# A one-layer hybrid decoder step: Pool's weight subtraction in halves, more store buffers, other pacer costs, ordering edges, and another scheduling simulation

## The chip, the cores and the metric

The kernel runs on one core of a Trainium2 chip. The metric is device microseconds of the whole program from launch to end. TensorE (PE) does the matrix products; VectorE (DVE), ScalarE (ACT) and GpSimd (POOL) do elementwise work; the DMAs that matter here are issued one after another by SyncE (SP). Each engine works through its own list of instructions in order and waits on semaphores for the others.

## The reference

One layer of a decoder for 2048 prompt tokens and 8 sequences of 8 new tokens, all in float32, model width 1024:

```python
h = rmsnorm(x, norm_attn)
p = h @ w_in                                   # 1024 -> q, k, v, 14 RWKV slices, 2048 gates
o_attn = attention(q, k, v)                    # sliding window of 128, with sinks
o_rwkv = rwkv7_mixer(p[..., e3:e4], ...)       # a linear recurrence over time, state 64 x 64 a head
merged = g1 * (o_attn @ w_branch_attn) + g2 * (o_rwkv @ w_branch_rwkv)
x = x + merged @ w_out
u = rmsnorm(x, norm_ffn) @ w_ffn_in            # 1024 -> 2 * 2816
f = (gelu(causal_conv3(gate)) * value) @ w_ffn_out
y = rmsnorm(x + f, norm_final)
```

The outputs are y for both sets of tokens and the new caches: window keys and values, the last RWKV row, the RWKV state and the last convolution rows.

## The kernel before, in words

**Tiling.** The 2112 tokens are three blocks of 704, each worked on in two halves of 384 and 320 columns (`HALF`). Activations lie with the channel on the 128 partitions. A float32 product is made from three products in a reduced float32 format: weights and activations are split in a high and a low part, and `mm3` (line 321) does high x high, low x high, high x low for each 128 rows of the contraction. One weight unit is 128 x 1024; `unit` (line 301) loads it into `wr` (two buffers), ACT copies it to the high part (L310), and for two units in three POOL, for the third DVE, subtracts to get the low part (L313) in `wp` (two buffers). A unit feeds 48 matmuls: three times eight, for each half.

**Stages.** `run` goes through: `inputs(0)` (the projections of block 0), `inputs(1)`, the merge of block 0 (`merge`: branch products, `w_out`, second norm), its feed-forward part (`ffn`), `inputs(2)`, merge and `ffn` of block 1, merge and `ffn` of block 2. These dense products are the foreground. Each half's product ends in a PSUM bank of the pool `psd` (three banks) that DVE or ACT empties: L767 and L772 in the projections, L1277 and L1303 in the merge, L1337 and L1344 (`up`, `gb`) and L1373 in `ffn`.

**The background.** Everything of a block that isn't a dense product is a Python generator, pushed onto a named stream. `prep` (stream r) forms the operands of the recurrence and ends in six PSUM evacuations (two of ACT into `kt`, then four of DVE into `m`), whose tiles share one tag with two buffers and are each stored by a DMA (L914 to L939). `rest(b)` (stream c) runs `inverse` twice (a triangular inverse: 31 pairs of DVE instructions L1016 and L1018, then five DVE transposes L1022 and L1027, then small matmuls), beside it the attention of the block, then the recurrence `chain` in 11 chunks and its group norm. `rest(0)` runs under `inputs(1)`, `rest(1)` and `rest(2)` under the two first `ffn` stages. `drain` forces out what is left of a stream where a stage needs its result.

**What sets the order.** Before each 128-row step of a dense product `mm3` calls `tick` (line 262), which offers every stream one step of its generator. The pacer decides by clocks of its own: `cost` (line 213) gives each traced instruction a price, `account` (line 236) adds it up for each engine, and `step` (line 268) goes on only if no engine's clock is more than `ROOM` ahead of PE's and if the stream's due time is past. A generator's `yield 0.2` sets the due time 0.2 us behind the modelled end of its step. So the pacer's prices set after which dense matmul each background instruction is traced. The library then puts each engine's instructions in order with a simulation of its own, by priority (the order of tracing) and readiness; an instruction that is ready earlier in the simulation may come ahead of one traced before it.

Of the kernel before, what the change touches and what calls it, by code (L numbers as in the profile page):

```python
# [17 lines left out]
P = 128  # L18
# [9 lines left out]

ROOM = {"DVE": 2.0, "Activation": 2.5, "Pool": 4.0}
LAG = tuple((j, h) for j in range(6) for h in range(2)) + ((6, 0), (7, 0), (6, 1), (7, 1))  # L30
# [72 lines left out]
class Kernel:  # L103
    def __init__(self, tc, i, o, es):
# [13 lines left out]
        self.clock = dict.fromkeys(("PE", "DVE", "Activation", "Pool"), 0.0)  # L118
        self.seen, self.chained = 0, 0.0

# [5 lines left out]

    def bank(self, k="r"):
        return self.pb[k].tile([P, 512], F32, tag="ps" + k, name="ps" + k)

# [82 lines left out]
    @staticmethod  # L212
    def cost(ins, engine):
        n = 1
        for _, k in ins.outs[0].ap[1:]:
            n *= k
        if engine == "PE":
            if ins.ins[0].dtype == F32R:
                return 0.013 + 0.00042 * n
            if ins.is_transpose or n <= 2:  # L220
                return 0.11
            return 0.01 + 0.00168 * n / (1 if min(ins.tile_size) == P else 2)
        kind = type(ins).__name__
        if engine == "Activation":
            return 0.19 + 0.00084 * n
        two = kind == "InstTensorTensor"
        if engine == "Pool":
            return 0.1 + (0.0024 if two else 0.0009) * n
        if kind == "InstStreamTranspose":
            return 0.06 + 0.002 * n  # L230
        full = [a for a in ins.ins if hasattr(a, "ap") and math.prod(k for _, k in a.ap[1:]) > 1]
        if len(full) > 1 and not any(a.bass_ap.tensor.name.startswith("ps") for a in full):
            return 0.1 + 0.0014 * n
        return 0.1 + (0.00105 if len(full) > 1 else 0.0009) * n

    def account(self):
# [4 lines left out]
        for k in range(self.seen, m):  # L241
            ins = new[k]
            engine = str(ins.engine).split(".")[-1]
            if engine not in t or not type(ins).__name__.startswith("Inst") or isinstance(ins, mybir.InstDMACopy):
                continue
            c = self.cost(ins, engine)
            if engine == "PE":
                t["PE"] += c
                self.chained = max(self.chained, t["PE"] + 0.1)
            else:  # L250
                t[engine] = max(t[engine], t["PE"]) + c
                self.chained = max(self.chained + c + 0.06, t[engine])
        self.seen = m
        return self.chained

    def push(self, stream, *gens):
        self.streams.setdefault(stream, deque()).extend([g, 0.0, 0.0] for g in gens)

    def tick(self):

        self.account()
        for q in self.streams.values():
            self.step(q)

    def step(self, q):
        t = self.clock
        if not q or q[0][1] > t["PE"] or any(t[e] - t["PE"] > r for e, r in ROOM.items()):
            return
        self.account()
        entry = q[0]  # L270
        self.chained = max(entry[2], t["PE"])
        try:
# [3 lines left out]
            w = None  # L276
        end = self.account()
        if isinstance(w, tuple):
            entry[1], entry[2] = w[0], 0.0
        else:  # L280
            entry[1], entry[2] = (0.0, end) if w is None else (end + w, 0.0)

    def together(self, *queues):

        qs = [deque([g, 0.0, 0.0] for g in q) for q in queues]
        while any(qs):
# [4 lines left out]
    def drain(self, *names):  # L291

        while any(self.streams.get(n) for n in names):
            self.account()
            for n in names:
                q = self.streams.get(n)
                if q:
                    self.clock["PE"] = max(self.clock["PE"], q[0][1], *(self.clock[e] - r for e, r in ROOM.items()))
                    self.step(q)
# [3 lines left out]
    def unit(self, src, w=None):  # L303
# [8 lines left out]
        self.nw += 1  # L312
        eng.tensor_tensor(w[:, 1], raw, w[:, 0].bitcast(F32), op=ALU.subtract)  # L313
        return w
# [504 lines left out]
    def prep(self, b, p, hf, xk, xv, xr, pp, st):  # L819
# [90 lines left out]
        for u in range(0, nch, 4):  # L910
# [3 lines left out]
            for c in range(k):  # L914
                nc.tensor.transpose(ps[:, c * 128:(c + 1) * 128], kb[:, u + c], self.cst("ident"))
            kt = pp.tile([P, 4, 128], F32, tag="m", name="kt", bufs=2)
            nc.scalar.copy(kt[:, :k].rearrange("p c j -> p (c j)"), ps[:, :k * 128])
            nc.sync.dma_start(self.kbd[b][hf][u:u + k, :, p].rearrange("c q j -> q c j"), kt[:, :k])

        for u in range(0, nch, 4):  # L920
# [8 lines left out]
            for r_ in range(2):  # L929
                ps = pss[r_]  # L930
                m = pp.tile([P, 4, 128], F32, tag="m", name="m", bufs=2)
                kpr = k
# [3 lines left out]
                if kpr:  # L936
                    nc.vector.tensor_tensor(m[:, :kpr], ps[:, :kpr * 128].rearrange("p (c j) -> p c j", j=128),  # L937
                                            self.cst("maskp").unsqueeze(1).to_broadcast([P, kpr, 128]), op=ALU.mult)
                nc.sync.dma_start(self.md[b][hf][u:u + k, :, p, r_].rearrange("c q j -> q c j"), m[:, :k])  # L939

    def headsum(self, sq, sel, least, eps, k):
# [42 lines left out]
    def inverse(self, b, hf, ip):  # L984
# [38 lines left out]
        for r in range(2):  # L1023
            o = 64 - r * 64
            for u in range(2):
                rows = slice(o + 32 * u, o + 32 * u + 32)
                nc.vector.transpose(q[rows, :, 32 * u:32 * u + 32].rearrange("p b t -> p t b"), qb[rows])  # L1027
            nc.gpsimd.memset(q[o + 32:o + 64, :, 0:32], 0.0)
# [488 lines left out]
    def rest(self, b):  # L1517

        with self.pool("att", side="right") as ap:
            att = [self.attn_prompt(b, ap)]  # L1520
            if b == NB - 1:
                att.append(self.attn_sample(ap))
            yield from self.together([self.inverse(b, hf, ap) for hf in range(2)], att)
        with self.pool("chain", 2, side="right") as kp:
# [162 lines left out]
```

## Time and profile before

| what | us |
|---|---|
| median of three runs | 3515.13 (3509.72 to 3517.71) |
| the profiled execution | 3505.69 |
| its span, first to last instruction | 3503.6 |
| PE busy | 3309.8 (94%) |
| DVE busy | 2061.3 (59%) |
| ACT busy | 1232.9 (35%) |
| POOL busy | 928.1 (26%) |

Idle time of PE is the span less its busy time. A group of instructions is given by its line, engine, operation, and written tile `<-` read tiles; `psd` is a foreground PSUM bank, `psr` and `psc` are background banks. A wait reads "engine tile line <- engine tile line": the instruction that stood still and the one that let it go. PEclk is the share of the full TensorE clock that was granted.

### The profile page before, as it was taken

What the parts mean: (1) busy time and instruction counts of PE and PEld (TensorE: products, weight loads), DVE (VectorE), ACT (ScalarE), POOL (GpSimd) and SP (SyncE); (2) the same over time, 40 slices, a digit from 0 to 9 for tenths busy, and PEclk for the clock granted to TensorE, in tenths of its full rate; (3) what the DMA queues carried; (4) which work ended last, traced back from release to release, by engine and by line L of the source; (5) the groups of instructions that cost most, each with busy time, mean ns of one, the idle gap of its engine ahead of it and who ended that gap; (6) DMA issues with size and microseconds to landing.
All of it is one profiled execution on the core that took longest, in us unless ns stands there. A gap on an engine that the chain in (4) does not pass through costs nothing.

```text
span 3503.6 us, 60421 instructions
## 1 busy us (share of the span) xinstructions
PE 3309.8 (94%) x24072; PEld 3163.1 (90%) x24072; DVE 2061.3 (59%) x4088; ACT 1232.9 (35%) x2276; POOL 928.1 (26%) x632
## 2 busy tenths in 40 slices
PE   8999899998989899999999998989999999999998
PEld 8889888887989889999899998988899999999997
DVE  6566777533567755575665256775455565555555
ACT  4233344522233462332333323355222323222223
POOL 3233232211332121122333243221212243122123
PEclk9999999998999999999999999999999999999999
DMA  4455354465432226432644642322632272222222
GB/s 129 129 164 152 112 136 141 116 203 181 140 90 79 72 82 182 142 106 67 199 128 137 192 143 75 84 76 82 183 113 95 81 239 89 67 67 68 72 67 72
DMA packets 341834, 416.02 MB, mean 119 GB/s; under 512 B 110896, under 2 KB 269488, under 8 KB 341296
## 3 DMA queue, kind: packets, MB, share of 16 engines
q1 hardware_dynamic: 337392, 406.39, 38.2%
q10 hardware_dynamic: 4160, 5.77, 0.5%
q8 instruction: 189, 3.10, 0.4%
q14 instruction: 93, 0.76, 0.1%
HBM read 314.63 MB, written 98.41 MB: 118 GB/s over the span
## 4 chain that ended last, share of the span: by engine, by line
PE 59%; DVE 11%; DMA 4%; issue 4%; ACT 2%; POOL 2%; SPq 1%; DVEq 0%; POOLq 0%; ACTq 0%
PE psd L326 51%; DVE qt L1016 2%; DVE cc L1347 2%; DVE qb L1018 1%; DVE qinv L1027 1%; POOL wp L313 1%; ACT wp L310 1%; DMA kbd<-kt 1%; DVE ff L318 1%; PE psr L678 1%; PE psr L630 1%; PE psc L1090 1%; DVE wp L313 1%; PE psc L1123 0%; PE psc L1120 0%
## 5 line engine op out<-in xcount | busy, mean ns | idle before, releaser
L326 PE MATMUL psd<-o,wp 128*128 128x320 f32 (+1 forms) x7488 | 1280.2, 329 | 61.8 <-DVE gb L1344 18.4
L326 PEld LDWEIGHTS psd<-o,wp 128*128 128x128 f32 x7488 | 1223.2, 191 | 85.2 <-issue 29.2
L326 PE MATMUL psd<-h,wp 128*128 128x384 f32 (+1 forms) x6336 | 1126.5, 332 | 34.5 <-ACT wp L310 13.9
L326 PEld LDWEIGHTS psd<-h,wp 128*128 128x128 f32 x6336 | 1037.3, 192 | 57.3 <-ACT wp L310 14.9
L313 POOL TENSOR_TENSOR wp<-wr,wp 128x1024 fp32r<-128x1024 f32 x236 | 572.0, 2424 | 1754.2 <-ACT wp L310 1587.0
L310 ACT CAST wp<-wr 128x1024 fp32r<-128x1024 f32 x354 | 371.4, 1049 | 578.3 <-PE psd L326 525.3
L326 PE MATMUL psd<-ff,wp 128*128 128x384 f32 (+1 forms) x3168 | 536.5, 326 | 4.6 <-DVE ff L318 2.7
L326 PEld LDWEIGHTS psd<-ff,wp 128*128 128x128 f32 x3168 | 511.5, 188 | 13.7 <-issue 5.8
L1373 DVE TENSOR_TENSOR x<-x,psd 128x320 f32<-128x320 f32 (+1 forms) x288 | 148.7, 519 | 227.1 <-PE psd L326 226.2
L1347 DVE SCALAR_TENSOR_TENSOR cc<-gb,pt,cc 128x704 f32<-128x704 f32 (+1 forms) x132 | 190.0, 1439 | 34.2 <-ACT cc L1345 32.9
L313 DVE TENSOR_TENSOR wp<-wr,wp 128x1024 fp32r<-128x1024 f32 x118 | 145.5, 1233 | 63.7 <-ACT wp L310 62.6
L1345 ACT ACTIVATE cc<-gb,pt 128x64 f32<-128x64 f32 (+2 forms) x154 | 96.2, 638 | 243.2 <-DVE gb L1344 233.4
L1344 DVE TENSOR_TENSOR gb<-psd,rb 128x64 f32<-128x64 f32 (+2 forms) x154 | 70.2, 469 | 169.7 <-PE psd L326 169.4
L318 DVE TENSOR_TENSOR ff<-cc,ff 128x384 fp32r<-128x384 f32 (+1 forms) x132 | 115.2, 875 | 43.2 <-ACT ff L317 43.1
L1356 ACT ACTIVATE cc<-cc 128x704 f32<-128x704 f32 x66 | 52.4, 794 | 177.7 <-DVE cc L1347 102.2
L367 POOL TENSOR_TENSOR acc<-acc,sq 128x320 f32<-128x320 f32 (+1 forms) x81 | 82.6, 1021 | 86.1 <-ACT sq L366 83.5
L317 ACT CAST ff<-cc 128x384 fp32r<-128x384 f32 (+1 forms) x132 | 63.9, 488 | 99.0 <-DVE cc L1359 97.9
L1337 DVE TENSOR_TENSOR up<-psd,rb 128x384 f32<-128x384 f32 (+1 forms) x132 | 68.5, 519 | 50.1 <-PE psd L326 50.1
L1283 DVE SCALAR_TENSOR_TENSOR h<-m,h 128x384 fp32r<-128x384 f32 (+1 forms) x48 | 51.9, 1081 | 66.3 <-ACT h L1282 66.3
L937 DVE TENSOR_TENSOR m<-psr,ct 128x512 f32<-128x512 f32 (+2 forms) x88 | 45.7, 539 | 76.0 <-DMA kbd<-kt 57.5
L1016 DVE TENSOR_TENSOR qt<-nb,qb 128x31 f32<-128x31 f32 (+15 forms) x186 | 85.7, 461 | 4.5
L1280 POOL TENSOR_TENSOR m<-m 128x384 f32<-128x384 f32 (+1 forms) x48 | 48.2, 1004 | 149.9 <-DVE m L1277 103.9
(256 smaller groups left out, 3274.1 us busy)
## 6 DMA issues: line engine op xcount, KB each, us to landing
wr<-in_w_fi SPq DMA_DIRECT2D x132, 512.0 KB, 3.5
wr<-in_w_in SPq DMA_DIRECT2D x108, 512.0 KB, 3.8
wr<-in_w_fo SPq DMA_DIRECT2D x66, 512.0 KB, 3.5
cm<-md SPq DMA_DIRECT2D x33, 512.0 KB, 4.7
gt<-gd SPq DMA_DIRECT2D x48, 352.0 KB, 3.5
md<-m SPq DMA_DIRECT2D x48, 256.0 KB, 2.8
wr<-in_w_br SPq DMA_DIRECT2D x24, 512.0 KB, 3.9
wr<-in_w_out SPq DMA_DIRECT2D x24, 512.0 KB, 3.5
```

The source lines that it names most:

```text
L310: nc.scalar.copy(w[:, 0], raw)
L313: eng.tensor_tensor(w[:, 1], raw, w[:, 0].bitcast(F32), op=ALU.subtract)
L317: self.nc.scalar.copy(hi, src)
L318: (eng or self.nc.vector).tensor_tensor(lo, src, hi.bitcast(F32), op=ALU.subtract)
L326: nc.tensor.matmul(ps[:, :n], w[:, a, wk * 128:(wk + 1) * 128], act[:, k0 + k, b, c0:c0 + n], start=(start and k == 0 and j == 0), stop=(s ...
L367: eng.tensor_tensor(acc, acc, sq[:, :n], op=ALU.add)
L1016: nc.vector.tensor_tensor(tv, nb[:, s + 1:, s:s + 1].to_broadcast([P, k, s + 1]), qb[:, s:s + 1, :s + 1].to_broadcast([P, k, s + 1]), op=A ...
L1337: nc.vector.tensor_tensor(up[:, c0:c0 + n], ps[:, :n], rb[:, c0:c0 + n], op=ALU.mult)
L1344: nc.vector.tensor_tensor(dst, view(ps, 0), view(rb, c0), op=ALU.mult)
L1345: nc.scalar.activation(view(c, c0), dst, ACT.Identity, bias=self.par("cb", f), scale=cw[2])
L1347: nc.vector.scalar_tensor_tensor(c[:, :npr], gb[:, u:u + npr], cw[u], c[:, :npr], op0=ALU.mult, op1=ALU.add)
L1373: nc.vector.tensor_tensor(xv, xv, ps[:, :n], op=ALU.add)
```

## The change

It has six parts.

1. POOL's subtraction of a weight unit is done in two instructions of 512 columns; DVE's stays one of 1024.
2. `kt` and `m` have four buffers for blocks 0 and 2; for block 1 the first pair of `m` keeps two, and `kt` and the second pair of `m` borrow the two tiles of the tag `xv`.
3. The pacer's prices change: ACT's fixed part falls from 0.19 to 0.12; DVE instructions with two full inputs cost 0.0012 a column wherever these lie; small matmuls cost in proportion to the used part of the array; matmuls of one or two columns cost 0.223. A DVE instruction that reads no PSUM and would begin during a POOL two-input instruction is priced to begin near that one's end. ACT's `ROOM` falls from 2.5 to 2.0.
4. The pacer waits for more: a step needs the second of the last three modelled ends of `psr` use to be past, each named wait is 0.3 longer, a stream can have a least distance between steps (1.4 for `inverse`), and the four transposes of L1027 each get a step of their own.
5. Every background instruction on DVE and ACT is ordered behind the last foreground instruction on its engine that reads `psd` and was traced before it. It is an order in the engine's list and no semaphore.
6. The library's ordering pass runs on its timeline simulation (`schedule_with_timeline_sim=True`) instead of its default one.

```diff
@@
-ROOM = {"DVE": 2.0, "Activation": 2.5, "Pool": 4.0}
+ROOM = {"DVE": 2.0, "Activation": 2.0, "Pool": 4.0}
...
+        self.anchor, self.inside = {}, False
+        self.seen, self.chained, self.free = 0, 0.0, deque([0.0] * 3, 3)
+        self.taken, self.locked = 0, (0.0, 0.0)
...
     def bank(self, k="r"):
+        self.taken += k == "r"
...
             if ins.ins[0].dtype == F32R:
-                return 0.013 + 0.00042 * n
-            if ins.is_transpose or n <= 2:
-                return 0.11
-            return 0.01 + 0.00168 * n / (1 if min(ins.tile_size) == P else 2)
+                return 0.0135 + 0.000417 * n
+            if ins.is_transpose:
+                return 0.11 * n / 128
+            if n <= 2:
+                return 0.223
+            return max(0.03, 0.01 + 0.00168 * n * math.prod(ins.tile_size) / (P * P))
...
-            return 0.19 + 0.00084 * n
+            return 0.12 + 0.00084 * n
...
-            return 0.06 + 0.002 * n
+            return 0.06 + 0.0019 * n
...
-        if len(full) > 1 and not any(a.bass_ap.tensor.name.startswith("ps") for a in full):
-            return 0.1 + 0.0014 * n
-        return 0.1 + (0.00105 if len(full) > 1 else 0.0009) * n
+        return 0.1 + (0.0012 if len(full) > 1 else 0.0009) * n
...
+            if engine in ("DVE", "Activation"):
+                if self.inside:
+                    if engine in self.anchor:
+                        self.tc.add_manual_dep(ins, self.anchor[engine], mybir.DependencyInfo(
+                            mybir.DependencyClass.NoSync, mybir.DependencyReason.DATA), reason="after the dense work before it")
+                elif any(hasattr(a, "bass_ap") and a.bass_ap.tensor.name.startswith("psd") for a in ins.ins):
+                    self.anchor[engine] = ins.name
...
-                t[engine] = max(t[engine], t["PE"]) + c
+                start = max(t[engine], t["PE"])
+                if engine == "Pool" and type(ins).__name__ == "InstTensorTensor":
+                    self.locked = start, start + c
+                elif engine == "DVE" and self.locked[0] <= start < self.locked[1] and not any(
+                        hasattr(a, "bass_ap") and a.bass_ap.tensor.name.startswith("ps") for a in ins.ins):
+                    start = self.locked[1] - 0.2
+                t[engine] = start + c
...
+    def open(self):
+        return max(self.free[1], *(self.clock[e] - r for e, r in ROOM.items()))
...
-        if not q or q[0][1] > t["PE"] or any(t[e] - t["PE"] > r for e, r in ROOM.items()):
+        if not q or q[0][1] > t["PE"] or self.open() > t["PE"]:
...
+        self.free.extend([end] * min(3, self.taken - taken))
...
-            entry[1], entry[2] = (0.0, end) if w is None else (end + w, 0.0)
+            entry[1], entry[2] = (0.0, end) if w is None else (end + w + 0.3, 0.0)
+        entry[1] = max(entry[1], at + entry[3])
...
-        eng.tensor_tensor(w[:, 1], raw, w[:, 0].bitcast(F32), op=ALU.subtract)
+        step = 1024 if eng is nc.vector else 512
+        for u in range(0, 1024, step):
+            sl = slice(u, u + step)
+            eng.tensor_tensor(w[:, 1, sl], raw[:, sl], w[:, 0, sl].bitcast(F32), op=ALU.subtract)
...
-            kt = pp.tile([P, 4, 128], F32, tag="m", name="kt", bufs=2)
+            kt = self.mtile(b, pp, "kt")
...
-                m = pp.tile([P, 4, 128], F32, tag="m", name="m", bufs=2)
+                m = self.mtile(b, pp, "m" if u == 0 else "kt")
...
+    def mtile(self, b, pp, name):
+        if b == 1 and name == "kt":
+            return self.tp.tile([P, 2, 384], F32, tag="xv", name="kt", bufs=2)[:].rearrange("p a c -> p (a c)")[:, :512].rearrange("p (c j) -> p c j", j=128)
+        return pp.tile([P, 4, 128], F32, tag="m", name=name, bufs=2 if b == 1 else 4)
...
             for u in range(2):
                 rows = slice(o + 32 * u, o + 32 * u + 32)
+                yield
                 nc.vector.transpose(q[rows, :, 32 * u:32 * u + 32].rearrange("p b t -> p t b"), qb[rows])
...
-            yield from self.together([self.inverse(b, hf, ap) for hf in range(2)], att)
+            yield from self.together((1.4, [self.inverse(b, hf, ap) for hf in range(2)]), (0.0, att))
...
-    with tile.TileContext(nc) as tc, ExitStack() as es:
+    with tile.TileContext(nc, schedule_with_timeline_sim=True) as tc, ExitStack() as es:
```

More of the change, by code (lines that the diff above doesn't have):

```diff
@@ L118, in __init__ @@
         self.clock = dict.fromkeys(("PE", "DVE", "Activation", "Pool"), 0.0)
-        self.seen, self.chained = 0, 0.0
+        self.anchor, self.inside = {}, False
+        self.seen, self.chained, self.free = 0, 0.0, deque([0.0] * 3, 3)
+        self.taken, self.locked = 0, (0.0, 0.0)
     def pool(self, name, bufs=1, **k):
@@ L254, in account, with push @@
         return self.chained
-    def push(self, stream, *gens):
-        self.streams.setdefault(stream, deque()).extend([g, 0.0, 0.0] for g in gens)
+    def push(self, stream, *gens, every=0.0):
+        self.streams.setdefault(stream, deque()).extend([g, 0.0, 0.0, every] for g in gens)
     def tick(self):
@@ L270, in step @@
         entry = q[0]
-        self.chained = max(entry[2], t["PE"])
+        self.inside = True
+        at, taken = t["PE"], self.taken
+        self.chained = max(entry[2], at)
         try:
@@ L277, in step @@
         end = self.account()
+        self.inside = False
+        self.free.extend([end] * min(3, self.taken - taken))
         if isinstance(w, tuple):
@@ L280, in step @@
         else:
-            entry[1], entry[2] = (0.0, end) if w is None else (end + w, 0.0)
+            entry[1], entry[2] = (0.0, end) if w is None else (end + w + 0.3, 0.0)
+        entry[1] = max(entry[1], at + entry[3])
     def together(self, *queues):
-        qs = [deque([g, 0.0, 0.0] for g in q) for q in queues]
+        qs = [deque([g, 0.0, 0.0, every] for g in q) for every, q in queues]
         while any(qs):
@@ L297, in drain @@
                 if q:
-                    self.clock["PE"] = max(self.clock["PE"], q[0][1], *(self.clock[e] - r for e, r in ROOM.items()))
+                    self.clock["PE"] = max(self.clock["PE"], q[0][1], self.open())
                     self.step(q)
```

## The prediction

> **What bounds the kernel now.** I read the page first: its header, the busy line and the slices of PE and of the granted clock.
>
> ```profile
> span 3503.6 us, 60421 instructions
> ...
> PE 3309.8 (94%) x24072; PEld 3163.1 (90%) x24072; DVE 2061.3 (59%) x4088; ACT 1232.9 (35%) x2276; POOL 928.1 (26%) x632
> ...
> PEclk9999999998999999999999999999999999999999
> ```
>
> PE sets the time: it is idle for 3503.6 - 3309.8 = 193.8 us. Nothing here removes a matmul, so the change can only take idle time of PE, and clock that is missing behind it, or add to them. The busy time by stage says where the idle time lies.
>
> ```profile
> core 0: us, PE busy (x) PEld busy (x) DVE busy (x) ACT busy (x) POOL busy (x), PEclk, DMA share, GB/s
> 340.00:885.00 545.00, 494.43 (x4139) 446.76 (x4137) 306.88 (x695) 209.75 (x472) 129.10 (x95) 0.95 0.51 150
> ...
> 2975.00:3503.00 528.00, 511.77 (x3174) 509.83 (x3173) 279.58 (x537) 153.88 (x223) 120.45 (x62) 0.99 0.22 69
> ```
>
> The first stretch is the projections of block 1 with the background of block 0: 50.6 us idle and 5% of the clock missing. The last one, block 2's feed-forward part without background, idles for 16.2 us, nearly all at its end. So the idle time comes with the background. The view of waits names it:
>
> ```profile
> PE psd L326 <- ACT wp L310: 30.4, 7, 9.8
> PE psr L927 <- DVE m L937: 20.0, 18, 2.3
> PE psd L326 <- DVE gb L1344: 18.4, 2, 9.7
> PE psd L326 <- DVE xs L767: 9.6, 2, 6.4
> PE psr L981 <- DVE nwyd L352: 9.2, 7, 2.8
> PE psd L326 <- ACT o L317: 9.0, 5, 4.9
> PE psd L326 <- POOL wp L313: 5.0, 4, 1.8
> PE psd L326 <- DVE up L1337: 4.6, 1, 4.6
> PE psr L817 <- DVE m L937: 2.2, 2, 1.1
> PE psr L678 <- DVE m L937: 2.1, 1, 2.1
> PE psr L866 <- DVE m L937: 1.9, 3, 1.3
> ```
>
> The numbers are microseconds in total, times, and the longest. DVE's lateness is behind most of them, though DVE is busy for only 59%: it is late in places, not overall.
>
> **The change part by part.**
>
> **The store buffers.** The four rows with `m` make 20.0 + 2.2 + 2.1 + 1.9 = 26.2 us. What holds `m` is seen from DVE, and in one place in the order of time (DVE, then PE, then PE's clock in two windows):
>
> ```profile
>   DMA kbd<-kt: 57.5, 17
>   DMA md<-m: 15.7, 15
> ```
>
> ```profile
> 185.88 1.29 DVE L937 TENSOR_TENSOR m<-psr,ct 128x512 f32<-128x512 f32 x2 [3.96 <-DMA kbd<-kt]
> ```
>
> ```profile
> 186.63 0.49 PE L927 MATMUL psr<-ar,kb 64*128 64x128 f32 x2 [1.74 <-DVE m L937]
> ```
>
> ```profile
> 186.60:188.30 1.70, 1.67 (x9) 1.55 (x10) 0.57 (x1) 0.00 (x0) 0.00 (x0) 1.00 0.88 292
> 188.30:191.70 3.40, 3.40 (x14) 3.40 (x13) 1.91 (x6) 1.87 (x4) 0.00 (x0) 0.50 0.85 235
> ```
>
> The first `m` needs the buffer of the first `kt`, whose store has not landed; DVE stands 3.96 us, PE fills the three `psr` banks and stops for 1.74 us. With four buffers the first pair of `m` takes the two that nobody holds, and the second pair comes to those of `kt` after two more evacuations; block 1, with its borrowed tiles, has four in effect too. The waits for `kt` (57.5 of the 73.2 us) go, those for `m`'s own stores mostly too. I take 80% of 26.2 us: 21. The bounds are 0 (DVE is late for another reason next) and 26.2.
>
> **What an idle microsecond costs beyond itself.** Behind that stop PE runs 3.40 us at half clock: 1.7 us more for 1.74 us idle. Behind a longer stop (next fence) it is 2.5 us, half of 5.0, for 9.69. So the factor on an idle microsecond lies between 1.26 and 1.98; the long stops hold more of the idle time, and I take 1.4. The store buffers then give 21 x 1.4 = 29 us. The Trainium skill ("TensorE: Matmul & The Clock Gate", section "What's actually happening") says that the clock falls to half after at least one idle window of about 3.4 us; by that these short stops would cost no clock and the term would be 21, the total 8 us later. The trace does not agree: half of that length was enough here.
>
> **The transposes.** Five of them stand in one step of `inverse`:
>
> ```profile
> 1158.22 7.60 DVE L1027 STREAM_TRANSPOSE qinv<-qb 32x1024 f32<-32x1024 f32 x4
> 1165.85 0.49 DVE L1344 TENSOR_TENSOR gb<-psd,rb 128x320 f32<-128x320 f32 x1
> ```
>
> ```profile
> 1166.49 3.86 PE L326 MATMUL psd<-o,wp 128*128 128x384 f32 x11 [9.69 <-DVE gb L1344]
> ```
>
> ```profile
> 1158.00:1166.00 8.00, 0.00 (x0) 0.00 (x0) 7.92 (x6) 0.00 (x0) 0.00 (x0) 0.70 0.00 2
> 1166.00:1171.00 5.00, 4.51 (x14) 4.54 (x15) 4.82 (x6) 1.59 (x2) 2.37 (x1) 0.50 0.00 0
> ```
>
> The evacuation of `gb` waits behind 7.60 us of transposes, all three `psd` banks are full, PE stops. This is both waits of the `gb` row (18.4 us). With a step for each transpose, 1.9 us, and the evacuation ahead of the background traced after it, `gb` can be late by one transpose, and three banks cover that. What is late next is the inverse itself, by the evacuations let through. I take 16 of 18.4 us, at this row's own factor of 1.26: 20 us (bounds 0 and 18.4 x 1.4 = 26).
>
> **Pacing and order elsewhere.** The other DVE rows on `psd`, `xs` and `up`, make 14.2 us. At one of them the inverse runs ahead of the evacuation:
>
> ```profile
> 391.39 2.27 DVE L1016 TENSOR_TENSOR qt<-nb,qb 128x87 f32<-128x87 f32 x1
> 393.69 0.25 DVE L1018 TENSOR_TENSOR qb<-qb,qt 128x87 f32<-128x87 f32 x1
> ```
>
> ```profile
> 395.09 10.13 PE L326 MATMUL psd<-h,wp 128*128 128x320 f32 x48 [6.44 <-DVE xs L767]
> ```
>
> The same shape takes 0.25 us or 2.27 us; the long one lies beside POOL's subtraction of 1024 columns. The pacer's old price knew nothing of that; the new one does, 1.4 us lie between steps, and the evacuation may no longer be overtaken by background traced behind it. But the inverses' work stays, and the work beside it too: I take half, 7 us x 1.4 = 10 (bounds 0 and 20). Ordering adds no semaphore. What queues behind an evacuation is background on DVE and ACT, and the background matmuls behind that; an evacuation waits for at most one half, some 4 us of matmuls, and only in the stretch from 340 to 885 is the background needed soon (costed below).
>
> **POOL's halves.** The subtraction, ACT's copy before it, POOL's nearest smaller instruction, and a stretch in which PE never stops:
>
> ```profile
> L313 POOL TENSOR_TENSOR wp<-wr,wp 128x1024 fp32r<-128x1024 f32 x236 | 572.0, 2424 | 1754.2 <-ACT wp L310 1587.0 <-DVE qt L1016 31.1 <-DVE chalo L1355 31.1
> L310 ACT CAST wp<-wr 128x1024 fp32r<-128x1024 f32 x354 | 371.4, 1049 | 578.3 <-PE psd L326 525.3 <-DMA wr<-in_w_in 17.1 <-issue 12.1
> L1280 POOL TENSOR_TENSOR m<-m 128x384 f32<-128x384 f32 x24 | 24.3, 1011 | 94.5 <-DVE m L1277 50.4 <-DMA gt<-gd 42.0 <-issue 2.0
> ```
>
> ```profile
> 3000.00:3400.00 400.00, 400.00 (x2489) 400.00 (x2488) 209.11 (x388) 114.35 (x160) 82.58 (x35) 1.00 0.22 69
> ```
>
> (2424 - 1011) / 640 = 2.21 ns a column, so 512 columns take some 1.29 us (an estimate from these two), a pair 2.59: 0.16 us more for each of 236 units, 38 us of POOL, hidden by its 1754.2 us of idle time ahead of this line. The low part comes 0.16 us later, and up to a DVE instruction more if one slips between. A unit feeds PE for 7.7 us (48 matmuls at 400 / 2489 us); its making takes 1.05 + 2.42 us: 4 us of slack hide it. Gain: a blocked DVE instruction waits 1.3 us instead of up to 2.4. Of the waits this touches chiefly the chains of tiny instructions (`nwyd`, 9.2 us): I take 3 us x 1.4 = 4 (bounds -5, as much again as the `POOL wp` row, and 13).
>
> **The slower background.** In the stretch from 340 to 885 nothing lies behind the background of block 0: its merge starts when the last gather is in. PE's wait, and the first and last starts of the inverse (L1016), the chain (L1082) and the gather's loads (L1241) in the stretch:
>
> ```profile
> 864.51 2.89 PE L326 MATMUL psd<-o,wp 128*128 128x384 f32 x6 [4.94 <-ACT o L317]
> ```
>
> ```profile
> L1016 DVE TENSOR_TENSOR qt<-nb,qb x62: 191/364/2486, 358.2 to 530.9; 128x31 f32<-128x31 f32 x4, 128x60 f32<-128x60 f32 x4, 128x87 f32<-128x87 f32 x4, 128x112 f32<-128x112 f32 x4
> ```
>
> ```profile
> L1082 PE MATMUL psc<-cvu,cm x176: 218/218/267, 721.1 to 828.4; 64*64 64x64 f32 x176
> ```
>
> ```profile
> L1241 SPq EVENT_SEMAPHORE  x7: 17/28/1096, 860.7 to 875.7; - x7
> ```
>
> The chain has 11 chunks with three named waits each, at 0.3 us: 10 us. The inverse and attention add perhaps ten more such waits on this path, 3 us. ACT's lower price gives some back (0.07 us for each instruction on a step's path), the bank rule takes some. I put the lengthening at 10 us, all of it paid (bounds -10 and 88, the latter below). In the feed-forward stages it is hidden by the dense work that follows the background.
>
> **The library's other order.** No row of this trace shows it. It may send any DMA, matmul or evacuation earlier or later. The nearest row is `ACT wp` (30.4 us in 7 waits: weight units late, as their loads or casts stood behind other work): at best it goes, at worst it comes three times over. Bounds -43 and +85 us, both with the factor 1.4; I take 0, since neither side has a row.
>
> Sum: 29 + 20 + 10 + 4 - 10 = 53 us. The profiled execution took 3505.7 us, so it becomes 3452.7. The runs' median lies 9.4 us above that execution, and I predict 3462 us, 1.5% less than 3515.1.
>
> **The rivals.**
>
> *The background becomes the bound of the stretch from 340 to 885* (slower). The new price of a 64 x 64 matmul is 0.037 us against 0.064; with 32 of them in a chunk the modelled PE clock advances 0.9 us less, so 0.9 us more of dense work goes in between, and 0.9 us of waits besides: 1.8 us on a chunk of 10.7 us (107.3 us for ten), 17%. If the whole background of 517 us (358.2 to 875.7) stretches so, the dense work is used up early and PE idles for 88 us more: 3515 + 88 - 63 = 3540. For it: the drain above already shows PE waiting for this gather. Against: PE stands for little of the chain, so less dense work in the old mixture was not what held it. It decides from 63 us on, a stretch of 12%.
>
> *The other order makes weight units late* (slower). 61 us more of `ACT wp` waits at 1.4 cost 85 us and outweigh the 53: 3547. Against: four microseconds of slack in each unit.
>
> *The stops only move* (the same). DVE's work under the inverses is what it was; if `gb`, `xs` and `up` wait as before and half of the store term comes, 15 - 10: 3510.
>
> *Most of it goes* (faster still). All rows of `m`, `gb`, `xs`, `up`, and half of `wp` and `nwyd` go: 26.2 + 18.4 + 14.2 + 19.8 = 78.6, times 1.4: 110 us, 3405.
>
> *The seam starves POOL.* Under the inverses DVE instructions follow each other without a pause; if each takes the turn ahead of POOL's second half, some 20 units are late by a microsecond or two past their slack: 30 us back, 3492.
>
> **How the numbers follow.** Chances: forecast 0.52, most of it goes 0.15, background as the bound 0.12, late weight units 0.09, stops only move 0.09, starved POOL 0.03. The forecast's own range, by its bounds, is 3435 to 3495. The range reaches to 3400 for the fast rival and to 3540 on the slow side, where the first slow rival lies and just short of the second. A difference under 0.2% can't be told from none for this kernel. Faster: 0.52 + 0.15 + 0.03 = 0.70; the same 0.08, nearly all of the stops that only move; slower 0.22.
>
> **What would show it.** *Stores*: the row of L937 has no `kbd<-kt` to speak of, and PE's waits for `m` fall from 26 to some 5 us. *Transposes*: no wait of PE for `gb` over 3 us. *POOL*: 472 instructions of some 1.29 us, and inverse pairs that take at most 1.5 us where they took 2.3. *Stretch*: its merge begins at 885 or a little later in its own time, with `ACT o` waits near 9 us; if these grow past 40 us, the first rival holds. *Order*: `ACT wp` near 30 us. *Sum*: PE idle near 150 us and granted clock above 0.95 in the stretch. I'd be wrong in the mechanism, not only in size, if PE's idle time does not fall, or if it falls and PE's busy time grows by as much.

## The result, and the profile after

The changed kernel takes 3411.93 us (median of four runs, 3406.49 to 3418.91) where the kernel before, run beside it, takes 3513.33 us. The ratio is 0.9712, with a 95% interval of 0.9687 to 0.9737: 2.9% less, 101 us. Predicted were 3462 us, with a range of 3400 to 3540. The sign and the range hold; the gain is nearly twice the 53 us of the forecast, and the time lies within 7 us of the rival "most of it goes" (3405).

The page of the changed kernel: header, busy line, and the slices of the granted clock.

```profile
span 3414.6 us, 60708 instructions
...
PE 3294.5 (96%) x24072; PEld 3164.2 (93%) x24072; DVE 1950.5 (57%) x4088; ACT 1239.6 (36%) x2286; POOL 1007.7 (30%) x870
...
PEclk9999999997999999999999999999999999999999
```

The number of matmuls is the same. PE's idle time falls from 193.8 to 3414.6 - 3294.5 = 120.1 us, by 73.7, and its busy time by 15.3: the granted clock over the span is 0.978 instead of 0.973. So between the two profiled executions each idle microsecond that went took 89.0 / 73.7 = 1.21 us with it. The one before was 7.6 us faster than the median of its runs, the one after 4.4 us slower; the medians differ by 101.4 us, which would make 1.38 if the idle times were the same there.

The view of PE's waits (total us, times, longest us):

```profile
PE psd L354 <- ACT wp L335: 23.4, 6, 8.2
PE psd L354 <- ACT o L345: 14.5, 4, 6.5
PE psd L354 <- DVE m L1313: 9.6, 2, 6.2
PE psr L1016 <- DVE nwyd L380: 9.3, 3, 5.3
PE psc L1161 <- ACT cvu L1129: 6.4, 11, 1.4
...
PE psd L354 <- DVE xs L795: 0.7, 1, 0.7
PE psr L693 <- DVE kt L965: 0.5, 1, 0.5
```

The dense matmul of L326 is now at L354, the evacuation of `m` (L937) at L965, where the second pair of `m` bears the name `kt`. The rows of `m` (26.2 us), `gb` (18.4) and `up` (4.6) are gone, that of `xs` has shrunk from 9.6 to 0.7. The largest rows that remain are ACT's copies for the dense matmuls (`wp`, `o`), an evacuation of the merge (L1313) and short instructions of the background.

The instructions of L965, with what ended DVE's idle time ahead of them (us, times):

```profile
  PE psr L955: 65.7, 36
  DMA kbd<-kt: 7.4, 4
```

DVE waited 57.5 + 15.7 us for the stores here; now 7.4, and for the rest it waits for PE, which has work.

The span can be cut at the first and the last evacuation of the `w_out` products of the three blocks, which stand at the same place of the program in both kernels:

| stretch | before, us | after, us | PE idle before | after |
|---|---|---|---|---|
| start to `w_out` of block 0 | 948 | 935 | 83 | 73 |
| to `w_out` of block 1 | 1078 | 1042 | 49 | 18 |
| to `w_out` of block 2 | 763 | 733 | 39 | 13 |
| the rest, without background | 534 | 530 | 19 | 16 |

Two stretches with background lose most of their idle time. The first one, which had the most, keeps most of it. Busy time by stretches of the first one:

```profile
core 0: us, PE busy (x) PEld busy (x) DVE busy (x) ACT busy (x) POOL busy (x), PEclk, DMA share, GB/s
340.00:737.00 397.00, 387.11 (x2854) 365.02 (x2852) 245.57 (x570) 175.61 (x400) 125.92 (x107) 0.99 0.48 139
737.00:874.00 137.00, 90.51 (x1144) 71.06 (x1141) 47.56 (x119) 25.82 (x64) 7.75 (x10) 0.73 0.53 165
```

And the same of the kernel before:

```profile
340.00:737.00 397.00, 363.94 (x2785) 335.45 (x2784) 257.30 (x581) 168.82 (x388) 106.91 (x80) 0.95 0.47 133
737.00:885.00 148.00, 130.48 (x1362) 111.32 (x1356) 49.58 (x114) 40.94 (x84) 22.19 (x15) 0.93 0.63 195
```

Up to 737 us the idle time falls from 33.1 to 9.9 us. Behind that the reverse: 17.5 us idle before, 46.5 us now, at a clock of 0.73. The projections' last instruction, ACT's gate, shows why (starts, first to last; L1234 before, L1270 after):

```profile
L1234 ACT ACTIVATE g<-psd,der x32: 514/544/587, 583.9 to 850.5; 128x384 f32<-128x384 f32 x16, 128x320 f32<-128x320 f32 x16
```

```profile
L1270 ACT ACTIVATE g<-psd,der x32: 507/546/586, 525.7 to 736.7; 128x384 f32<-128x384 f32 x16, 128x320 f32<-128x320 f32 x16
```

The dense work of this stage is used up 114 us earlier, the background of block 0 isn't, and PE goes through its chain, group norm and gather almost alone. The merge's first evacuation (`m`) starts at 872.4 us instead of 884.7. What this first stretch saves of idle time it saves before 340 us (16.5 us idle, 32.1 before); from there to the merge's first evacuation 55.8 us are idle instead of 50.3, at a clock of 0.92 instead of 0.95.

### The profile page after: what moved, and what is told of

It is laid out like the page before. It is cut to its first block, busy times and chain, and to the rows that moved or that the text cites. A ratio compares the mean times of both kernels' runs of the same rounds, so it can differ in the third digit from the quotient of the medians.

```text
span 3414.6 us, 60708 instructions
## 1 busy us (share of the span) xinstructions
PE 3294.5 (96%) x24072; PEld 3164.2 (93%) x24072; DVE 1950.5 (57%) x4088; ACT 1239.6 (36%) x2286; POOL 1007.7 (30%) x870
## 4 chain that ended last, share of the span: by engine, by line
PE 72%; DVE 3%; DMA 2%; ACT 2%; issue 1%; POOL 1%; SPq 0%; POOLq 0%; DVEq 0%; ACTq 0%
PE psd L354 62%; PE psr L955 1%; PE psr L706 1%; DMA cvu<-vvd 1%; PE psc L1161 1%; PE psc L1159 1%; PE psc L982 1%; PE psc L1126 1%; PE psc L1156 1%; PE psr L658 1%; PE psr L693 1%; PE psc L1118 0%; PE psc L1255 0%; DMA gt<-gd 0%; PE psc L1153 0%
## 5 line engine op out<-in xcount | busy, mean ns | idle before, releaser
L354 PE MATMUL psd<-o,wp 128*128 128x320 f32 (+1 forms) x7488 | 1271.9, 327 | 40.4 <-ACT o L345 14.5
L354 PEld LDWEIGHTS psd<-o,wp 128*128 128x128 f32 x7488 | 1215.0, 190 | 59.1 <-ACT o L345 16.4
L341 POOL TENSOR_TENSOR wp<-wr,wp 128x512 fp32r<-128x512 f32 x472 | 653.7, 1406 | 1609.4 <-ACT wp L335 1439.1
L354 PE MATMUL psd<-h,wp 128*128 128x384 f32 (+1 forms) x6336 | 1096.2, 327 | 14.4 <-ACT wp L335 9.8
L354 PEld LDWEIGHTS psd<-h,wp 128*128 128x128 f32 x6336 | 1020.5, 189 | 29.3 <-ACT wp L335 10.3
L354 PE MATMUL psd<-ff,wp 128*128 128x384 f32 (+1 forms) x3168 | 536.5, 325 | 0.5 <-DVE x L1409 0.4
L354 PEld LDWEIGHTS psd<-ff,wp 128*128 128x128 f32 x3168 | 509.1, 188 | 8.3 <-issue 3.2
L1409 DVE TENSOR_TENSOR x<-x,psd 128x384 f32<-128x384 f32 (+1 forms) x288 | 147.9, 518 | 206.1 <-PE psd L354 205.1
L1383 DVE SCALAR_TENSOR_TENSOR cc<-gb,pt,cc 128x704 f32<-128x704 f32 (+1 forms) x132 | 170.1, 1288 | 37.3 <-ACT cc L1381 36.5
L346 DVE TENSOR_TENSOR ff<-cc,ff 128x384 fp32r<-128x384 f32 (+1 forms) x132 | 92.0, 698 | 40.9 <-ACT ff L345 40.3
L1313 DVE SCALAR_TENSOR_TENSOR m<-gt,psd 128x384 f32<-128x384 f32 (+1 forms) x96 | 49.2, 518 | 74.8 <-PE psd L354 55.9
L1270 ACT ACTIVATE g<-psd,der 128x384 f32<-128x384 f32 x64 | 35.4, 553 | 130.3 <-PE psd L354 85.3
L1395 DVE TENSOR_TENSOR cc<-cc,up 128x384 f32<-128x384 f32 (+1 forms) x132 | 71.2, 541 | 20.0 <-ACT cc L1392 16.3
```

The costliest lines, as they stand in the source:

```text
L341: eng.tensor_tensor(w[:, 1, sl], raw[:, sl], w[:, 0, sl].bitcast(F32), op=ALU.subtract)
L346: (eng or self.nc.vector).tensor_tensor(lo, src, hi.bitcast(F32), op=ALU.subtract)
L354: nc.tensor.matmul(ps[:, :n], w[:, a, wk * 128:(wk + 1) * 128], act[:, k0 + k, b, c0:c0 + n], start=(start and k == 0 and j == 0), stop=(s ...
L1383: nc.vector.scalar_tensor_tensor(c[:, :npr], gb[:, u:u + npr], cw[u], c[:, :npr], op0=ALU.mult, op1=ALU.add)
L1395: nc.vector.tensor_tensor(cv, cv, up[:, c0:c0 + n], op=ALU.mult)
L1409: nc.vector.tensor_tensor(xv, xv, ps[:, :n], op=ALU.add)
```

## The experiments

Each run is given by its ratio to the kernel before on the same chip, and by span and idle time of PE in its profiled execution. An interval is some 0.2 to 0.3% to either side, so a difference of two ratios is known to 0.3 or 0.4%, 10 to 14 us. Span and idle time are those of one execution each, and executions of one kernel differ: the 13 runs of the kernel before beside the buffers' run had a granted clock of 0.962 to 0.969, its profiled execution 0.973.

| kernel | ratio (95%) | span | PE idle |
|---|---|---|---|
| the changed kernel | 0.9712 (0.9687 to 0.9737) | 3414.6 | 120.1 |
| before + new buffers | 0.9860 (0.9845 to 0.9874) | 3472.0 | 170.7 |
| before + timeline simulation | 0.9878 (0.9858 to 0.9897) | 3472.1 | 164.9 |
| before + a step for each transpose | 1.0003 (0.9989 to 1.0017) | 3526.8 | 191.0 |
| changed - buffers | 0.9698 (0.9682 to 0.9714) | 3416.5 | 121.8 |
| changed - buffers - bank rule | 0.9724 (0.9704 to 0.9743) | 3418.8 | 120.5 |
| changed - timeline simulation | 0.9755 (0.9725 to 0.9786) | 3428.4 | 146.4 |
| changed - POOL's halves | 0.9757 (0.9742 to 0.9771) | 3432.7 | 130.2 |
| changed - longer waits | 0.9763 (0.9745 to 0.9780) | 3431.1 | 133.8 |
| changed - ordering edges | 0.9825 (0.9803 to 0.9847) | 3457.2 | 149.5 |
| changed - edges - timeline simulation | 0.9847 (0.9827 to 0.9867) | 3461.8 | 168.9 |
| changed - edges - new prices | 0.9913 (0.9892 to 0.9933) | 3488.9 | 172.3 |
| changed, short waits in the first stage | 0.9716 (0.9690 to 0.9743) | 3414.5 | 123.1 |

**The store buffers.** First the part alone, then the change without it.

```diff
 before + new buffers
-            kt = pp.tile([P, 4, 128], F32, tag="m", name="kt", bufs=2)
+            kt = self.mtile(b, pp, "kt")
...
-                m = pp.tile([P, 4, 128], F32, tag="m", name="m", bufs=2)
+                m = self.mtile(b, pp, "m" if u == 0 else "kt")
 changed - buffers: the same two lines the other way round
```

> The kernel before with the changed kernel's buffers for kt and m as its only change. Theory of the prediction: 29 us off, 3480 to 3490 us. Rival (the stops only move to the next late thing): 3505 us or more.

> The changed kernel with kt and m back on one tag with two buffers in all blocks. Theory of the prediction (the store term is 29 us): 3436 to 3446 us, with DVE m <- DMA kbd<-kt back at some 50 us and PE <- DVE m at some 20 us. Rival (new prices and the bank rule space the evacuations out, so that two buffers would do): 3412 to 3420 us.

Alone the buffers take 47 us off (3520.51 to 3473.20), more than the 29 forecast. PE's wait for `m` at L927 falls from 20.0 to 2.6 us. Taken out of the changed kernel they cost nothing that can be measured (0.9698 against 0.9712). This was unexpected, and its trace says how it can be. What DVE waits for ahead of L965 in the changed kernel without the buffers:

```profile
  DMA md<-m: 32.3, 27
  DMA kbd<-kt: 42.5, 16
```

and the one wait of PE for it:

```profile
PE psr L845 <- DVE m L965: 2.2, 1, 2.2
```

DVE is as late as it was before the change (74.8 us here, 73.2 there), but PE no longer notices. One place in the order of time, the same kernel:

```profile
155.95 1.60 PE L955 MATMUL psr<-ar,kb 64*128 64x128 f32 x20
157.48 3.42 PE L354 MATMUL psd<-h,wp 128*128 128x320 f32 x20
158.02 1.29 DVE L965 TENSOR_TENSOR m<-psr,ct 128x512 f32<-128x512 f32 x2 [3.16 <-DMA kbd<-kt]
...
160.83 0.71 PE L955 MATMUL psr<-ar,kb 64*128 64x128 f32 x4
```

DVE stands 3.16 us for a store, as at 185.88 us in the trace of before. There 3 dense matmuls lay between the products that filled the last bank and the next product that needs one, and PE stopped for 1.74 us. Here 20 dense matmuls (3.42 us) lie there. The stop went because the consumer was placed later, not because the producer came sooner.

**What places it later.** The new rule on `psr` banks was one candidate, the timeline simulation the other.

```diff
 changed - buffers - bank rule (beside the two lines of the buffers)
     def open(self):
-        return max(self.free[1], *(self.clock[e] - r for e, r in ROOM.items()))
+        return max(*(self.clock[e] - r for e, r in ROOM.items()))
 before + timeline simulation
-    with tile.TileContext(nc) as tc, ExitStack() as es:
+    with tile.TileContext(nc, schedule_with_timeline_sim=True) as tc, ExitStack() as es:
```

> The changed kernel with two buffers for kt and m and without the bank rule. Theory (with four buffers gone nothing was lost, because the bank rule holds the next step back until the evacuations are done): without both PE waits for DVE m again by 10 us or more, and the time is 3435 us or more. Rival (other prices and waits space the steps already): 3412 to 3422 us, no row of PE <- DVE m above 3 us.

> The kernel before with the timeline simulation as its only change. Theory of the prediction (the other order is worth nothing by itself; stores, transposes and pacing carry the gain): 3500 to 3525 us. Rival (the order carries the half of the 101 us gained that the prediction had no term for): about 3460 us, with fewer ACT wp and DVE xs waits on PE. If the old pacing fits the timeline simulation badly it is slower than before, above 3525 us.

Without the bank rule PE's waits for `m` come to 2.5 + 2.0 + 1.0 + 0.6 = 6.1 us, a quarter of the 26.2, and the time is the same within what can be told (0.9724). So the rule is not what stands in for the buffers. The simulation alone, put into the kernel before with its two buffers, takes 43 us off. Its waits ahead of L937 (first line DVE's, second PE's, from the view of waits):

```profile
DVE m L937 <- DMA md<-m: 38.1, 24, 5.8
...
PE psr L927 <- DVE m L937: 2.3, 3, 1.0
```

DVE still waits for stores, PE's stop has gone from 20.0 to 2.3 us. The other order does it, on a kernel in which nothing else was changed. It moves other stops too: PE's wait for `gb` falls from 18.4 to 4.5 us, and those for `xs` and `up` rise from 14.2 to 29.1. That the order is also what stands in for the buffers in the changed kernel is likely, but not shown: the changed kernel without both was not tried. How the library's simulation arrives at that order was not looked into.

**The transposes.**

```diff
 before + a step for each transpose
                 rows = slice(o + 32 * u, o + 32 * u + 32)
+                yield
                 nc.vector.transpose(q[rows, :, 32 * u:32 * u + 32].rearrange("p b t -> p t b"), qb[rows])
```

> The kernel before with the four transposes in steps of their own as its only change. Theory of the prediction: 20 us off, 3490 to 3497 us, no wait of PE for DVE gb above 3 us. Rival (without the order edges the transposes still run ahead of the evacuation): 3508 us or more, with the two waits of 9 us still there.

The time doesn't change (1.0003). The wait the step was meant for falls from 18.4 to 2.7 us:

```profile
PE psr L927 <- DVE m L937: 19.8, 18, 2.2
PE psd L326 <- DVE xs L767: 12.4, 3, 6.5
...
PE psd L326 <- DVE wp L313: 10.2, 4, 8.3
...
PE psr L665 <- DVE kk L907: 6.1, 1, 6.1
...
PE psd L326 <- DVE gb L1345: 2.7, 2, 1.9
```

But more of `wp` from DVE (10.2 us for 2.1), of `kk` (6.1 for 4.1) and of `xs` (12.4 for 9.6) stand in its place, and the idle time is 191.0 for 193.8 us. A step of its own may shift everything traced after it against the dense work; that this is why other stops came was not shown. The opposite, the changed kernel with its transposes in one step, was not tried. Every run that leaves another part out of the changed kernel keeps PE's wait for `gb` at 2.1 us or less, so none of the others by itself is needed for that; what the step is worth there in time stays open.

**The ordering edges and the simulation, taken out.**

```diff
 changed - ordering edges
-            if engine in ("DVE", "Activation"):
+            if engine in ():
                 if self.inside:
 changed - timeline simulation
-    with tile.TileContext(nc, schedule_with_timeline_sim=True) as tc, ExitStack() as es:
+    with tile.TileContext(nc) as tc, ExitStack() as es:
```

> The changed kernel without the ordering edges on background instructions. Theory of the prediction (pacing elsewhere, edges included, is worth 10 us): 3415 to 3425 us. Rival (background overtaking evacuations is what makes DVE late, so the edges carry the surplus): 3450 us or more, with PE waiting for DVE gb, up and xs again.

> The changed kernel with the library's default simulation. Theory of the prediction: 3400 to 3425 us, as the changed kernel. Rival (the order carries half): about 3460 us. The rows to look at: PE's waits for ACT wp (23.4 us in the changed kernel), and the stretch up to the merge of block 0.

> The changed kernel without both. If the two are independent, its loss is the sum of the two single losses; if the edges make the simulation's order unimportant (or the other way round), it loses clearly more than that sum, since each covers for the other. Theory of the prediction: 3415 to 3435 us. Rival: 3470 us or more.

Without the edges 40 us come back (0.9825 - 0.9712 = 1.13%), without the simulation 15 (0.43%, just clear of the noise), without both 47 (1.35%), within the noise the sum of the two. Of the parts left out alone the edges are the dearest. PE's waits without them:

```profile
PE psr L1016 <- DVE nwyd L380: 13.0, 4, 5.7
PE psd L354 <- DVE wp L341: 11.2, 5, 4.6
PE psr L706 <- DVE pT L700: 9.4, 4, 7.1
PE psd L354 <- DVE xs L795: 6.4, 4, 4.3
...
PE psr L658 <- DVE mx L610: 5.7, 2, 4.6
...
PE psd L354 <- DVE up L1373: 3.7, 1, 3.7
...
PE psd L354 <- DVE gb L1380: 2.1, 1, 2.1
```

`xs`, `up` and `gb` are back, with 12.2 us, and beside them `wp`, `pT` and `mx`, that is background and weight units. No row is large. The loss is 12, 17 and 14 us in the three stretches with background.

**The prices.** Without the edges, for the old prices with the edges kept were not tried.

```diff
 changed - edges - new prices
-ROOM = {"DVE": 2.0, "Activation": 2.0, "Pool": 4.0}
+ROOM = {"DVE": 2.0, "Activation": 2.5, "Pool": 4.0}
...     cost() as before, and no price for POOL's lock:
-                    start = self.locked[1] - 0.2
+                    pass
```

> The changed kernel with the old prices (and ACT's old room), and without the order edges; to be compared with the run without the edges alone (3459 us). Theory (the prices, POOL's lock among them, keep DVE from being overbooked): 3475 us or more. Rival (prices hardly matter beside waits and edges): 3452 to 3466 us.

0.9913 against 0.9825 for the kernel that lacks the edges alone: the prices are worth 0.88%, some 30 us. The wait of PE for `pT` goes from 9.4 to 20.4 us and that for `up` from 3.7 to 10.0; 18 us are lost in the first stretch and 12 in the third.

**The longer waits.**

```diff
 changed - longer waits
-        return max(self.free[1], *(self.clock[e] - r for e, r in ROOM.items()))
+        return max(*(self.clock[e] - r for e, r in ROOM.items()))
...
-            entry[1], entry[2] = (0.0, end) if w is None else (end + w + 0.3, 0.0)
+            entry[1], entry[2] = (0.0, end) if w is None else (end + w, 0.0)
...
-            yield from self.together((1.4, [self.inverse(b, hf, ap) for hf in range(2)]), (0.0, att))
+            yield from self.together((0.0, [self.inverse(b, hf, ap) for hf in range(2)]), (0.0, att))
 changed, short waits in the first stage
-            entry[1], entry[2] = (0.0, end) if w is None else (end + w + 0.3, 0.0)
+            entry[1], entry[2] = (0.0, end) if w is None else (end + w + self.more, 0.0)
...     with self.more = 0.0 around inputs(1), and 0.3 elsewhere
```

> The changed kernel with the pacer's old waiting rules (no bank rule, no 0.3 us on named waits, no least distance for the inverse); the new prices stay. Theory, new after the first eight runs (the waiting rules took over what the buffers alone would give, and they space the background in the feed-forward stages): about 3440 us, the loss in the stages from the w_out product of block 0 on, PE <- DVE m small, since four buffers are there. Rival (prices and edges do it, the waits only delay the background): 3412 us or less, with an earlier merge of block 0.

> The changed kernel without the 0.3 us on named waits while block 0's background runs under the projections of block 1, where the merge waits for the background. Theory (the longer waits lie on that stage's path, 10 us or so): 3395 to 3407 us, the merge of block 0 some 5 to 15 us earlier. Rival (the matmuls and banks set that stage's pace, not the waits): 3408 to 3416 us.

With the old waits the kernel is 0.51% slower, 18 us. It loses 18 us in the third stretch (751 for 733) and is 5 us shorter in the first (930 for 935). So the waits do cost the first stage something, and pay elsewhere. But giving back the 0.3 us there alone brings 4 us in its length (931) and nothing in the time (0.9716), and the end of the stage looks as it did:

```profile
737.00:874.00 137.00, 91.78 (x1116) 72.12 (x1114) 46.52 (x117) 25.77 (x63) 9.84 (x12) 0.73 0.52 164
```

The background of block 0 has nearly the same length, whatever the waits: from the inverse's first instruction to the last load of the gather 502.9 us, with the old waits 496.4, with short waits in the first stage 498.3, in the kernel before 519.0. Within it the parts trade: with the old waits the inverse takes 147 us (from its first start to its last) and the chain 118, with the longer waits 264 and 87. The chain's matmuls of the changed kernel, which the prediction shows for the kernel before as 721.1 to 828.4:

```profile
L1118 PE MATMUL psc<-cvu,cm x176: 218/218/311, 730.8 to 817.3; 64*64 64x64 f32 x176
```

A chunk takes 5.0 to 6.8 us where the dense work is used up; with the old waits it takes 14.2 to 14.8 us beside the dense work and 5.0 to 5.2 behind it. So a chain that begins late is mostly made up for once PE has nothing else to do. Nor does the end of the dense work set the merge: in the kernel before with the new buffers it lies at 829 us, with short waits in the first stage at 728, and the merge's first evacuation starts at 864 and 868 us. What sets it stays open.

**POOL's halves.**

```diff
 changed - POOL's halves
-        step = 1024 if eng is nc.vector else 512
+        step = 1024
```

> The changed kernel with POOL's subtraction in one piece of 1024 columns. Theory of the prediction (4 us): 3411 to 3420 us. Rival (blocked DVE instructions are behind many late evacuations): 3430 us or more. DVE's busy time should rise from 1950 towards 2060 us in either.

Without the halves 0.45% are lost, 16 us. Its page's busy line:

```profile
PE 3302.5 (96%) x24072; PEld 3166.6 (92%) x24072; DVE 2030.4 (59%) x4088; ACT 1240.9 (36%) x2288; POOL 925.1 (27%) x632
```

DVE, whose instructions are the same in number, is busy for 80 us more (2030.4 for 1950.5): it is blocked for longer behind POOL's whole subtractions. The instructions that grow read no PSUM, as those of `ff` (L346, 937 ns in the mean for 698), while an evacuation such as L1409 takes 518 ns in both. PE's idle time is 10 us more.

## Why the prediction was right, and where not

**What bounds the kernel** was read rightly: no matmul went, PE's idle time fell, a part of the clock came back with it (0.973 to 0.978), and nearly all of it in stretches with background. The mechanism's own test, idle time down and busy time not up by as much, came out as stated. The sign for the stretch from 340 us, a clock above 0.95, did not: it is 0.92.

**The store buffers** (29 us): the step from DVE's wait to PE's stop is right, and alone the part gives more than that, 47 us, past its bound of 26.2 x 1.4 = 37. The idle part was sized well: 23.1 us went between the profiled executions, for 21 forecast, and their spans differ by 31.6. The rest of the 47 lies in the clock and in the kernel before's spread, whose profiled execution ran at 0.973 and its other runs here at 0.962 to 0.969. In the changed kernel it gives nothing, since something else in it already removes the same stop from its other end. The prediction had priced each part against the trace of before and added them up; for this part the sum has no place.

**The idle factor** (1.4): 1.21 between the profiled executions, nearer to the row of the long stop (1.26), and 1.38 by the medians if the idle times hold for them. So the runs don't decide against 1.4.

**The transposes** (20 us): this step failed. The stop at `gb` went as described, and with it no time; the rival "the stops only move" describes this part, alone. In the changed kernel the stop is gone; whether it would have moved without the other parts' help can't be told. DVE at such a place:

```profile
1235.06 2.01 DVE L1063 STREAM_TRANSPOSE qinv<-qb 32x1024 f32<-32x1024 f32 x1
1237.10 1.23 DVE L341 TENSOR_TENSOR wp<-wr,wp 128x1024 fp32r<-128x1024 f32 x1
1238.24 0.55 DVE L1409 TENSOR_TENSOR x<-x,psd 128x384 f32<-128x384 f32 x1
1238.82 2.02 DVE L1063 STREAM_TRANSPOSE qinv<-qb 32x1024 f32<-32x1024 f32 x1
1240.87 0.95 DVE L1409 TENSOR_TENSOR x<-x,psd 128x320 f32<-128x320 f32 x2
```

The evacuations (L1409) stand between the transposes, one late by at most one of them.

**Pacing and order elsewhere** (10 us): this term was sized wrongest. It took half of two rows of waits, `xs` and `up`. At the margin the edges are worth 40 us, the prices some 30 (without the edges), the longer waits 18. What they remove are many waits of 2 to 10 us that move from row to row between the kernels, so no row of the kernel before shows how much of them there is. What shows it is the sum of the idle time in the stages with background, 83 + 49 + 39 us, of which the prediction priced only the rows that it could name. That sum is a bound and no forecast: the first stage kept 73 of its 83 us.

**The library's other order** (0 us): wrong as a choice, within its bounds. Alone it takes 43 us off, the far end of -43 to +85; in the changed kernel 15. The nearest row taken, `ACT wp`, was not what it chiefly acts on: alone it takes this row from 30.4 to 20.9 us, but that of `m` from 26.2 to 2.9 and that of `gb` from 18.4 to 4.5. In the changed kernel `ACT wp` is even shorter without it (12.8 us for 23.4).

**POOL's halves** (4 us): right in sign, 16 us in size, past the bound of 13. The group of the halves:

```profile
L341 POOL TENSOR_TENSOR wp<-wr,wp 128x512 fp32r<-128x512 f32 x472 | 653.7, 1406 | 1609.4 <-ACT wp L335 1439.1
```

The median of one is 1294 ns, as estimated (1.29 us); the mean is 1406, so POOL's pieces now wait at times. The prediction credited the chains of `nwyd` alone, whose row hasn't changed (9.2 and 9.3 us); the gain is DVE's 80 us of busy time, in all that it does. That the inverse's pairs would take at most 1.5 us is wrong, by an instruction that the change leaves whole:

```profile
1102.59 2.40 POOL L346 TENSOR_TENSOR q<-q,q 128x1024 fp32r<-128x1024 f32 x1 [7.20 <-ACT q L345]
```

```profile
1102.75 2.33 DVE L1051 TENSOR_TENSOR qt<-nb,qb 128x60 f32<-128x60 f32 x1
```

POOL's subtraction for the attention's `q` still has 1024 columns, and a DVE instruction of 60 columns (0.22 us in most places) lasts as long as it does. The Trainium skill ("SBUF — State Buffer", section "Who interferes with whom") calls the contention between these two engines an exclusive lock, which a DVE instruction with two SBUF inputs meets beside a GpSimd instruction that reads SBUF; the trace agrees.

**The slower background** (-10 us): right in sign, half in size, and not by the path that was named. Against the old waits the longer ones cost that stretch 5 us (935 for 930) and lengthen the background by 6.5 (502.9 for 496.4). They were to lengthen the chain by 10 us, but it is shorter with them (86.5 us for 118.3, and 107.3 before the change), since it runs where the dense work is used up; what they lengthen is the inverse. The merge of block 0 starts 12 us earlier instead of 10 later, for the stretch gains more by the other parts. The prediction's chunk of 10.7 us was a mean that holds the 36 us between the two halves; most chunks before took 6 to 8. Yet what the rival "the background becomes the bound" describes is there in part: the dense work is used up 114 us early, and the 23 us of idle time saved between 340 and 737 us are outweighed by 29 us more behind it. The price stayed far from the rival's 88 us, for the background got no longer; its last load starts at 864.6 us where it started at 877.3 (the prediction's 875.7 is the queue's last wait for a semaphore, not a load).

**The sum.** Forecast 53, measured 89 between the two profiled executions and 101 between the medians. Neither way of adding the parts gives it: the ones tried alone make 47 + 43 + 0 without the edges, prices, waits and halves, and what is lost when one is taken out makes 0 + 15 + 40 + 30 + 18 + 16 = 119.

## What to carry to other kernels

A row of waits names one meeting of a late producer and an early consumer; with fixed engine lists the same stop can be taken away at either end, so two parts of a change may each be worth their full price alone, and one of them nothing beside the other. Bound such a change by the idle time of the stage, not by the rows that can be named, and test each part both alone and by leaving it out. Where a stage's end hangs on its background, look at what is left when the dense work is used up: here the dense work was used up 114 us earlier, and the next stage began only 12 us earlier.

## What the runs showed of the hardware

The clock can fall at half-busy work without any long stop. The second fence shows three of the stretches of half clock in the changed kernel, the first the pieces ahead of the first two of them:

```profile
763.40:766.90 3.50, 2.71 (x84) 2.46 (x82) 1.27 (x3) 0.37 (x1) 0.00 (x0) 1.00 0.62 150
766.90:770.30 3.40, 1.76 (x42) 1.35 (x37) 1.27 (x3) 1.35 (x4) 0.02 (x1) 0.99 0.91 275
818.00:821.50 3.50, 2.23 (x50) 1.75 (x48) 1.30 (x4) 0.91 (x3) 0.00 (x0) 1.00 0.04 9
821.50:825.00 3.50, 2.01 (x5) 0.93 (x5) 0.00 (x0) 2.35 (x8) 2.20 (x3) 0.98 0.00 0
```

```profile
770.30:787.40 17.10, 12.69 (x40) 9.04 (x40) 4.65 (x18) 4.50 (x11) 4.24 (x5) 0.50 0.19 55
825.00:842.00 17.00, 13.11 (x45) 10.00 (x45) 7.59 (x25) 1.95 (x6) 1.21 (x2) 0.50 0.12 39
845.60:866.00 20.40, 9.14 (x27) 7.36 (x28) 5.63 (x12) 5.38 (x13) 0.00 (x0) 0.50 0.76 267
```

PE was busy for 2.71 / 3.50 = 77% and 64% of the pieces that kept the clock, and for 52% and 57% of those behind which it fell, though the idle time there lies in gaps of at most about a microsecond. The stretches at half clock last 17.1, 17.0 and 20.4 us, five, five and six times 3.4 us. Three shorter stretches in this stage, from 732.7, 739.5 and 811.2 us, stand behind pieces of 3.41 us with PE busy for 58%, 40% and 53%. The busy share of a piece doesn't decide alone, though: elsewhere in this trace a stop of 2.83 us, which lies across two pieces with PE busy for 55% and 61% (from 616.6 us), cost no clock, and the clock fell behind two pieces that show PE busy throughout (from 1490.5 and 2296.0 us), both with many matmuls of 2 or 32 columns; the ends of matmuls in a trace are modelled. So no threshold can be given, but a stage in which PE goes through short dependent products lost clock here beside its idle time: 0.73 from 737 to 874 us. The Trainium skill ("TensorE: Matmul & The Clock Gate", section "What's actually happening") names at least one idle window of about 3.4 us for it; the length fits the stretches, but a piece that was only about half idle was enough here.
